# Padding the operand buffers of the matmuls by 32 and 64 bytes in a two-layer hybrid decoder trunk

## The chip, the cores and the metric

The kernel runs on one core of one Trainium2 chip. The metric is device time in microseconds (us) of one execution, from the first to the last instruction, as a median over runs.

## The reference

The reference computes two layers on 512 tokens of width 1,024, all in float32. Layer 0 normalises, projects once, and splits the result between a chunked state space scan (16 heads of 64) and a sliding-window attention (16 query heads, 2 key heads, window 128); both are projected back by one matrix. Layer 1 has a causal convolution module (width 31) in that place. Each layer ends in a gated feed-forward part of width 2,816 with a short convolution between its up-projection and its activation.

```python
def conv_ffn(h, w_up, conv_w, conv_b, w_down):
    u = causal_depthwise_conv(h @ w_up, conv_w, conv_b)
    return (jax.nn.silu(u[..., :D_FF]) * u[..., D_FF:]) @ w_down

for i in range(DEPTH):
    hn = rms_norm(h, mix_norm_w[i])
    if i % 2 == 0:
        proj = hn @ hyb_w_in[j]
        y_a = ssd_mixer(proj[..., :IN_A], ...)
        y_b = swa_sink_attention(proj[..., IN_A:], ...)
        mix = jnp.concatenate([y_a, y_b], axis=-1) @ hyb_w_out[j]
    else:
        mix = conformer_conv_module(hn, ...)
    h = h + mix
    h = h + conv_ffn(rms_norm(h, ffn_norm_w[i]), ffn_w_up[i], ...)
```

## The kernel before

Activations are held transposed: 128 channels on the partitions, 512 tokens along the free dimension, eight such tiles for the width of 1,024. Four phases run in turn, each with a pool of its own for its buffers: mix (layer 0's mixer), ffn0, conf (the convolution module), ffn1. Buffers that all phases use (tags in the set base, L78: wr, wh, wl, xr and some smaller ones) come from a shared pool; sbt (L81) picks the pool and hands out the next buffer of a tag. A tag has a fixed number of buffers of one size, placed one behind the other, and is used in rotation.

Large products keep float32 accuracy with three fast matmuls in place of one. Every operand is split into a rounded high part and the rest: a weight tile of 128 x 1,024 arrives in wr by DMA (wload, L124), ACT writes its high part to wh and DVE the rest to wl (wsplit, L118, three buffers each). Norm.split (L179) does the same for the normalised activations, with 16 buffers xr: high and low of row block 0, then of row block 1, and so on. The feed-forward part writes its gated activations as pairs of g (L782 to L785, 44 buffers). The attention's outputs are pairs of att (L684 to L687, 16 buffers); the state space half's outputs are pairs of xr (L732 to L735).

gemm (L131) runs over the row blocks of one weight tile and issues three matmuls for each:

```python
for i, (xh, xl) in enumerate(ops):
    c = slice(i * P, (i + 1) * P)
    TE.matmul(bank, wh[:, c], xh, start=first and i == 0, stop=False)
    TE.matmul(bank, wh[:, c], xl, start=False, stop=False)
    end = TE.matmul(bank, wl[:, c], xh, start=False, stop=last and i == n - 1)
```

They are lines 136, 137 and 138 of the profile. Each has 128 x 128 weights (the first argument after the bank) and a moving operand of 128 x 512. The up-projections (ffn, L756) use xr and go over 44 weight tiles of eight row blocks per layer; the down-projections use g and have eight output tiles of 22 row blocks per layer. The input projection of the mixer uses xr, its output projection att and then xr. The convolution module uses xr for its first projection and, for its second, dg, pr and g of its own pool (outputs, L1015, and gemm).

The order of work is set by the tile scheduler from the order of the program, with weight loads and splits pulled ahead (L127), except at the start of mix and in conf, where the order is written by hand. DMAs of weights go through SP's queue.

Of the kernel before, what the change touches and what calls it, by code (L numbers as in the profile page):

```python
# [14 lines left out]
P = 128  # L15
# [45 lines left out]
def kernel(ctx: ExitStack, tc: tile.TileContext, x, w_in, w_dt, w_out,  # L61
# [12 lines left out]
    def nm(s):  # L74
        uid[0] += 1
        return f"{s}_{uid[0]}"

    base = {"wr", "wh", "wl", "xr", "nsum", "nsq", "nvar", "nr", "nrb", "cv", "ct", "th"}  # L78
    phase = [sb]

    def sbt(tag, bufs, n=T, dt=F32, shape=None):  # L81
        pool = sb if tag in base else phase[0]
        return pool.tile(shape or [P, n], dt, name=nm(tag), tag=tag, bufs=bufs)

    BANKS = {"mm": 3, "pa": 2, "pb": 2, "pc": 1}
# [20 lines left out]
    def prm(name, i=None, n=1):  # L106
        group, o, w = PARAMS[name]
        t = ptiles[group]
        return t[:, o : o + w] if i is None else t[:, o + i : o + i + n]
# [8 lines left out]
    def wsplit(raw, n):  # L118
        wh, wl = sbt("wh", 3, RING, F32R), sbt("wl", 3, RING, F32R)
        S.copy(wh[:, :n], raw[:, :n])  # L120
        V.tensor_tensor(wl[:, :n], raw[:, :n], f32(wh[:, :n]), op=ALU.subtract)  # L121
        return wh, wl

    def wload(src):  # L124
        n = src.shape[-1]
        raw = sbt("wr", 3, RING)
        with tc.high_priority(offset=AHEAD):  # L127
            nc.sync.dma_start(raw[:, :n], src)
            return wsplit(raw, n)
# [43 lines left out]
    class Norm:  # L173
# [5 lines left out]
        def split(self, k):  # L179
            w = prm(self.wname, k)  # L180
            xh = sbt("xr", 16, T, F32R)
            S.activation(xh, h[k], AF.Copy, scale=w)
            xl = sbt("xr", 16, T, F32R)
            V.scalar_tensor_tensor(xl, h[k], w, f32(xh), op0=ALU.mult, op1=ALU.subtract)
            self.ops[k] = (xh, xl)
# [39 lines left out]
    def mixer(norm, nxt):  # L225
# [81 lines left out]
                V.tensor_copy(dst.rearrange("p j c e -> p c e j"), src.rearrange("p (c e j) -> p c e j", c=NB, e=2))  # L307
            return cs, et, dtj, ddj

        # the first tiles of the projection, fed tile by tile as x arrives  # L310
        first, ws, banks = [], [], {}
        with tc.manual_schedule():
            warm = mk([P, 1], "warm")
# [107 lines left out]
        V.tensor_scalar(nsink, prm("sink"), -1.0, None, op0=ALU.mult)  # L421
        chw = mk([P, 60], "chw")
        V.tensor_scalar(chw, prm("scw", 0, 60), 0.5, None, op0=ALU.mult)
        # convolved channels of the state space heads
        def conv_silu(i, dst):
            v = scaled(proj(), rb)
            t = sbt("ct", 2)
            conv_taps(t, v, None, 0, 4, chw[:, 48 + i : 49 + i], lambda k: chw[:, i * 4 + k : i * 4 + k + 1])
            th = sbt("th", 1)
            S.activation(th, t, AF.Tanh)  # L430
            V.scalar_tensor_tensor(dst, th, 1.0, t, op0=ALU.add, op1=ALU.mult)
# [83 lines left out]
            V.scalar_tensor_tensor(xs[j], xs[j], prm("sd", j), yd, op0=ALU.mult, op1=ALU.add)  # L515
            G.tensor_tensor(xs[j][:, P:], xs[j][:, P:], ec[:, P:], op=ALU.add)

        # keys, values, queries
        kraw = sbt("bc", 4)
        vfm = sbt("bc", 4)  # L520
        qraw = [None] * 8
# [90 lines left out]
            V.tensor_tensor(kla[half], kt[0:64], f32(kha[0:64]), op=ALU.subtract)  # L612
            V.tensor_tensor(klb[half], kt[64:P], f32(khb[64:P]), op=ALU.subtract)

        # attention
        head = {}
        yb = []

# [80 lines left out]
            if i >= LAG:  # L699
                attn_values(*units[i - LAG])  # L700

        # gates
        gs = [sbt("bc", 4) for _ in range(2)]
        for j in range(8):
            v = scaled(proj(), rb)
# [5 lines left out]
            g = j // 4  # L711
# [474 lines left out]
    for i, p in enumerate(phases):  # L1186
        a, b = norms[i], norms[i + 1]
        with tc.tile_pool(name=p, bufs=1) as pool:
            phase[0] = pool
            if p != "mix":  # L1190
                pload(p, pool)
            if p == "mix":
                mixer(a, b)
            elif p == "conf":
                conformer(a, b)
            else:
                l = int(p[-1])
                ffn(a, b, (w_up0, w_up1)[l], (w_dn0, w_dn1)[l], l)
# [105 lines left out]
```

## Time and profile before

| | |
|---|---|
| median of 2 runs | 1336.11 us (1335.57 to 1336.65) |
| profiled execution, its span | 1336.0 us |
| DMA moved | 125.08 MB, mean 94 GB/s |
| mean granted TensorE clock | 0.990 |

The profile gives, for each engine, its busy time, the groups of instructions by source line with their mean duration and the idle time before them, the chain of work that ended last, and a timeline with the start of each instruction. Durations of matmuls overlap, since the next one starts while the present one drains; the distance between two starts is read from the timeline. PE is TensorE's matmul row, PEld its row of weight loads. A tile's name in a row is that of its tag.

### The profile page before, as it was taken

The page shows a single profiled execution, that of the slowest core. Times are in us where ns is not written, and L with a number is a line of the kernel's source. Part 1 is how long each engine was busy: PE and PEld are TensorE (multiplying, and loading weights), DVE is VectorE, ACT ScalarE, POOL GpSimd, SP SyncE. Part 2 cuts the span into 40 slices and gives each one's busy share as a digit, 9 for nine tenths or more (in the row PEclk, how much of TensorE's full clock was granted, in tenths as well). Part 3 has the DMA queues.
Part 4 walks back from the last instruction along what each step waited for, and adds up shares of the span by engine and source line. Part 5 has one row for each costly group of instructions (what it writes and reads, how often), then busy time and mean ns, then how long its engine had stood idle before and what let it go on. Part 6 is the DMA issues. An engine that isn't in the chain of part 4 may idle for free.

```text
span 1336.0 us, 17056 instructions
## 1 busy us (share of the span) xinstructions
PE 1298.3 (97%) x6480; PEld 1040.7 (78%) x6480; DVE 884.8 (66%) x1430; ACT 541.3 (41%) x855; POOL 226.5 (17%) x264
## 2 busy tenths in 40 slices
PE   9999999999999999999999999687999999999998
PEld 7877777778888888888888866556888888888887
DVE  6976759985348777777323368897667777774221
ACT  5465537863234333333222244324633433332120
POOL 0031214540210000000000176672500000000000
PEclk9999999999999999999999999889999999999999
DMA  6212212212333333333233273532232233333331
GB/s 214 96 48 63 64 64 64 64 34 78 95 98 95 95 95 97 99 103 89 87 103 88 87 196 109 133 87 91 79 96 96 95 95 95 96 94 106 104 114 38
DMA packets 41553, 125.08 MB, mean 94 GB/s; under 512 B 4864, under 2 KB 7936, under 8 KB 41472
## 3 DMA queue, kind: packets, MB, share of 16 engines
q1 hardware_dynamic: 40752, 123.46, 30.0%
q8 instruction: 51, 0.84, 0.2%
q10 hardware_dynamic: 720, 0.55, 0.2%
q14 instruction: 30, 0.25, 0.1%
HBM read 119.64 MB, written 4.35 MB: 93 GB/s over the span
## 4 chain that ended last, share of the span: by engine, by line
PE 84%; DVE 9%; POOL 3%; ACT 2%; issue 2%; DMA 1%; POOLq 0%; ACTq 0%; DVEq 0%
PE mm L136 24%; PE mm L137 24%; PE mm L138 24%; DVE g L888 3%; POOL yp L903 1%; PE pb L506 1%; PE pc L681 1%; PE pb L672 1%; DVE wl L851 1%; DVE g L961 1%; PE pa L870 1%; PE pa L137 1%; PE pa L138 1%; PE pa L136 1%; PE pc L513 0%
## 5 line engine op out<-in xcount | busy, mean ns | idle before, releaser
L136 PE MATMUL mm<-xr,wh 128*128 128x512 f32 (+1 forms) x1136 | 442.4, 389 | 0.9 <-ACT wh L847 0.9
L138 PE MATMUL mm<-xr,wl 128*128 128x512 f32 (+1 forms) x1136 | 439.3, 387 | 2.7 <-DVE wl L851 2.7
L137 PE MATMUL mm<-xr,wh 128*128 128x512 f32 (+1 forms) x1136 | 439.4, 387 | 0.0
L120 ACT CAST wh<-wr 128x1024 fp32r<-128x1024 f32 (+1 forms) x178 | 183.6, 1032 | 466.0 <-PE mm L137 422.5
L121 DVE TENSOR_TENSOR wl<-wr,wh 128x1024 fp32r<-128x1024 f32 (+1 forms) x178 | 214.4, 1204 | 163.9 <-ACT wh L120 158.8
L136 PEld LDWEIGHTS mm<-xr,wh 128*128 128x128 f32 x1136 | 214.2, 189 | 47.3 <-issue 4.7
L138 PEld LDWEIGHTS mm<-xr,wl 128*128 128x128 f32 x1136 | 214.1, 189 | 46.3 <-DVE wl L851 2.9
L137 PEld LDWEIGHTS mm<-xr,wh 128*128 128x128 f32 x1136 | 214.3, 189 | 42.1 <-issue 0.6
L137 PE MATMUL mm<-g,wh 128*128 128x512 f32 x368 | 145.0, 394 | 0.0
L222 DVE TENSOR_TENSOR cv<-mm,nrb 128x512 f32<-128x512 f32 x114 | 78.2, 689 | 96.4 <-PE mm L138 91.6
L138 PE MATMUL mm<-g,wl 128*128 128x512 f32 x352 | 138.7, 394 | 0.0
L136 PE MATMUL mm<-g,wh 128*128 128x512 f32 x352 | 138.7, 394 | 0.0
L217 DVE SCALAR_TENSOR_TENSOR ct<-cv,par_ffn,ct 128x510 f32<-128x510 f32 (+1 forms) x176 | 131.0, 747 | 3.5 <-issue 0.4
L194 POOL TENSOR_TENSOR nsum<-nsum,nsq 128x512 f32<-128x512 f32 x21 | 34.0, 1617 | 433.0 <-ACT nsq L193 433.0
L137 PEld LDWEIGHTS mm<-g,wh 128*128 128x128 f32 x368 | 68.8, 187 | 17.0
L136 PEld LDWEIGHTS mm<-g,wh 128*128 128x128 f32 x352 | 65.8, 187 | 16.4
L138 PEld LDWEIGHTS mm<-g,wl 128*128 128x128 f32 x352 | 65.8, 187 | 16.2
L214 ACT ACTIVATE ct<-cv,par_ffn 128x512 f32<-128x512 f32 x88 | 71.4, 813 | 3.2 <-DVE cv L222 3.0
L903 POOL TENSOR_TENSOR yp<-yp,pr 128x512 f32<-128x512 f32 x36 | 59.9, 1664 | 37.4 <-ACT pr L902 35.8
L780 ACT ACTIVATE th<-ct 128x512 f32<-128x512 f32 x44 | 27.8, 632 | 84.5 <-DVE ct L217 84.5
L888 DVE SCALAR_TENSOR_TENSOR g<-u,par_conf,g 128x512 f32<-128x512 f32 x42 | 56.2, 1337 | 1.1
L791 DVE TENSOR_TENSOR h<-h,mm 128x512 f32<-128x512 f32 x16 | 11.0, 688 | 59.1 <-PE mm L138 59.1
(344 smaller groups left out, 1519.4 us busy)
## 6 DMA issues: line engine op xcount, KB each, us to landing
wr<-w_up SPq DMA_DIRECT2D x88, 512.0 KB, 3.5
wr<-w_in SPq DMA_DIRECT2D x29, 512.0 KB, 3.6
wr<-w_dn SPq DMA_DIRECT2D x32, 448.0 KB, 3.3
wr<-pw SPq DMA_DIRECT2D x24, 512.0 KB, 3.6
wr<-w_out SPq DMA_DIRECT2D x16, 512.0 KB, 3.6
wr<-w_dn SPq DMA_DIRECT2D x16, 512.0 KB, 3.5
u<-du SPq DMA_DIRECT2D x24, 262.0 KB, 4.7
u<-du SPq DMA_DIRECT2D x16, 140.0 KB, 2.9
```

Source lines behind the costliest of these rows:

```text
L120: S.copy(wh[:, :n], raw[:, :n])
L121: V.tensor_tensor(wl[:, :n], raw[:, :n], f32(wh[:, :n]), op=ALU.subtract)
L136: TE.matmul(bank, wh[:, c], xh, start=first and i == 0, stop=False)
L137: TE.matmul(bank, wh[:, c], xl, start=False, stop=False)
L138: end = TE.matmul(bank, wl[:, c], xh, start=False, stop=last and i == n - 1)
L194: eng.tensor_tensor(self.sum, self.sum, sq, op=ALU.add)
L214: S.activation(t, v, AF.Identity, bias=bias, scale=w(taps - 1))
L217: V.scalar_tensor_tensor(t[:, s:], v[:, : T - s], w(k), t[:, s:], op0=ALU.mult, op1=ALU.add)
L222: V.tensor_tensor(v, bank, rb, op=ALU.mult)
L780: S.activation(sg, c, AF.Silu)
L888: V.scalar_tensor_tensor(y[j], win(j, k), w(j, k), cvp[j, None] if k == ks[0] else y[j], op0=ALU.mult, op1=ALU.add)
L903: G.tensor_tensor(yp[j], yp[j], pr, op=ALU.add)
```

## The change

sbt adds a few float32 columns to each buffer of five tags, 8 (32 bytes) or 16 (64 bytes), and returns the buffer without them. Buffers of the pool of the convolution module are left as they are; xr, wh and wl come from the shared pool and are padded in every phase. The rest of the diff turns comment lines into empty ones.

```diff
+    STAGGER = {"xr": 8, "g": 8, "att": 8, "wh": 8, "wl": 16}
+
     def sbt(tag, bufs, n=T, dt=F32, shape=None):
         pool = sb if tag in base else phase[0]
+        extra = 0 if pool.name == "conf" else STAGGER.get(tag, 0)
+        if extra and shape is None:
+            return pool.tile([P, n + extra], dt, name=nm(tag), tag=tag, bufs=bufs)[:, :n]
         return pool.tile(shape or [P, n], dt, name=nm(tag), tag=tag, bufs=bufs)
```

## The prediction

> **What bounds the kernel now.** I read the page's busy times, the chain of work that ended last, the groups of instructions by form, and then the timeline for the starts of single matmuls.
>
> ```profile
> PE 1298.3 (97%) x6480; PEld 1040.7 (78%) x6480; DVE 884.8 (66%) x1430; ACT 541.3 (41%) x855; POOL 226.5 (17%) x264
> PE 84%; DVE 9%; POOL 3%; ACT 2%; issue 2%; DMA 1%; POOLq 0%; ACTq 0%; DVEq 0%
> L136 PE MATMUL mm<-xr,wh 128*128 128x512 f32 x1088 | 427.9, 393 | 0.0
> L137 PE MATMUL mm<-g,wh 128*128 128x512 f32 x368 | 145.0, 394 | 0.0
> L137 PE MATMUL mm<-att,wh 128*128 128x512 f32 x48 | 20.2, 422 | 0.0
> L136 PE MATMUL mm<-xr,wh 128*128 128x256 f32 x48 | 14.4, 301 | 0.9 <-ACT wh L847 0.9
> 410.00:610.00 200.00, 200.00 (x884) 165.62 (x883) 156.46 (x205) 78.50 (x93) 0.00 (x0) 1.00 0.32 98
> ```
>
> TensorE is busy 97% of the span and holds 84% of the chain. The last row (busy PE, PEld, DVE, ACT, POOL of 200 us, then the granted clock) shows a stretch of the feed-forward up-projection: TensorE never pauses, DVE is busy 78%. So the time is the number of matmuls times the distance from one start to the next. The 393 ns in the groups is not that distance, because matmuls overlap. The timeline has it:
>
> ```profile
> 499.92 0.39 PE L138 MATMUL mm<-xr,wl 128*128 128x512 f32 x1
> 499.92 0.19 PEld L136 LDWEIGHTS mm<-xr,wh 128*128 128x128 f32 x1
> 500.15 0.39 PE L136 MATMUL mm<-xr,wh 128*128 128x512 f32 x1
> ...
> 501.05 0.39 PE L137 MATMUL mm<-xr,wh 128*128 128x512 f32 x1
> ...
> 689.80 0.39 PE L137 MATMUL mm<-g,wh 128*128 128x512 f32 x1
> ...
> 691.20 0.39 PE L137 MATMUL mm<-g,wh 128*128 128x512 f32 x1
> ...
> 291.00 0.40 PE L138 MATMUL mm<-att,wl 128*128 128x512 f32 x1
> ...
> 296.13 0.39 PE L136 MATMUL mm<-att,wh 128*128 128x512 f32 x1
> ...
> 301.50:306.00 4.50, 4.50 (x12) 3.46 (x11) 4.32 (x12) 2.02 (x4) 0.00 (x0) 0.50 0.17 66
> ...
> 301.32 0.63 PE L138 MATMUL mm<-att,wl 128*128 128x512 f32 x1
> ...
> 306.02 0.63 PE L137 MATMUL mm<-att,wh 128*128 128x512 f32 x1
> ```
>
> Five gaps from 499.92 to 501.05 are 1.13 us, 226 ns at the rows' 10 ns of rounding; the stretch above counts 884 matmuls in 200 us, two of them at its edges, which is 226.7 ns each. Six gaps on g tiles are 1.40 us: 233.3 ns. Twenty-two on att tiles are 5.13 us: 233.2 ns. The shape, the line and the clock (1.00) are the same, so where the operands lie in memory is worth 6.6 ns, 3%. At half the clock (0.50 in the window's row) eleven gaps are 4.70 us, 427.3 ns, and half of that is 213.6 ns: what a matmul would take at full clock with nothing in its way. So 226.7 holds 13 ns of stall and 233.3 holds 20. The weights of the next matmul are read while the present one streams (499.92 beside 499.92).
>
> **Which addresses match.** The compiled program of the kernel before puts xr at byte 47,392 of each partition, wh at 80,160, wl at 92,448, g at 123,360, att at 124,736, and each further buffer 2,048 or 4,096 on. Modulo 256 that is 32, 32, 32, 224 and 64: xr starts where its weights start, g and att do not. The conformer's last products test this with the moving tiles (dg, pr, g, all at 192) left alone and the weights changed:
>
> ```profile
> 947.83 0.39 PE L137 MATMUL mm<-g,u 128*128 128x512 f32 x1
> ...
> 950.55 0.39 PE L137 MATMUL mm<-g,u 128*128 128x512 f32 x1
> ...
> 951.25 0.40 PE L137 MATMUL mm<-g,u 128*128 128x512 f32 x1
> ...
> 956.13 0.40 PE L137 MATMUL mm<-g,u 128*128 128x512 f32 x1
> ...
> 957.05 0.40 PE L138 MATMUL mm<-dg,wl 128*128 128x512 f32 x1
> ...
> 960.57 0.40 PE L138 MATMUL mm<-dg,wl 128*128 128x512 f32 x1
> ...
> 974.42 0.40 PE L137 MATMUL mm<-xr,wh 128*128 128x512 f32 x1
> ...
> 976.51 0.39 PE L137 MATMUL mm<-xr,wh 128*128 128x512 f32 x1
> ...
> 977.87 0.39 PE L137 MATMUL mm<-xr,wh 128*128 128x512 f32 x1
> ```
>
> Weights at 192 too: 12 gaps in 2.72 us, 226.7 ns. Weights at 64: 21 gaps in 4.88 us, 232.4. Weights at 32: 15 gaps in 3.52 us, 234.7. So an equal residue gives 226.7, and the four unequal pairs seen give 232.4 to 234.7, 233.4 in the mean. The last three rows add something: after a break, even the equal pair xr with wh first takes 9 gaps in 2.09 us, 232.2 ns, and only then 6 gaps in 1.36 us, 226.7. The low figure is a rhythm that a row of identical matmuls settles into.
>
> **The change part by part.** No instruction, wait or DMA is added, removed or moved; the slices [:, :n] keep every shape. What moves is where tiles start. (a) xr buffers lie 2,080 bytes apart, so buffer k starts at 32+32k modulo 256; wh (three buffers, b = 0 to 2) at 32+32b, wl at 128+64b. Within one gemm the moving tile now goes +32 (xh to xl), -32 (back), +64 (next row block), so the pair changes at nearly every matmul. For lines 136 and 138 the pair is equal in a quarter of the matmuls at b = 0 and 2 and never at b = 1; for line 137 in a quarter; together about one in five. (b) g, by the same rule, starts at 0+32k in the feed-forward phases, att at 96+32k. (c) Tiles behind wl in the shared pool move on by 800 bytes, 32 modulo 256; the conformer's own u, dg and g keep their distances to one another and shift against wh.
>
> Price of (a), bounds first. Nothing in the trace shows a rotating pair. The best end is the settled 226.7 (no loss), the worst the dearest fixed pair, 234.7. I take 232.2, the row it is nearest to: the pair that has not settled, since a pair that changes each time has no rhythm to settle into. The one equal pair in five is then no relief, for it comes singly. Of the 3,312 matmuls of 512 columns on xr (3 x 1,088, and 48 more in the output projection), 2,112 are the up-projections (88 weight tiles x 24) in unbroken rows at 226.7: 2,112 x 5.5 ns = +11.6 us. The other 1,200 are often broken by small matmuls; nine at 232.2 and fifteen at 226.7 in a tile of 24 would be 228.8 at worst, none broken 226.7; I take 228: 1,200 x 4.2 = +5.0 us. Price of (b): 1,056 matmuls on g (2 x 22 x 24), 233.3 to 232.2, -1.2 us; 192 on att, -0.2 us. The 144 of 256 columns on xr:
>
> ```profile
> 932.28 0.28 PE L1022 MATMUL mm<-pr,wl 128*128 128x256 f32 x1
> 932.39 0.28 PE L1020 MATMUL pc<-pr,xh 128*128 128x256 f32 x1
> ...
> 934.16 0.28 PE L1020 MATMUL mm<-dg,wh 128*128 128x256 f32 x1
> ...
> 935.46 0.28 PE L1022 MATMUL pc<-dg,xl 128*128 128x256 f32 x1
> ```
>
> Eleven gaps in 1.30 us, 118 ns, for a mixed row; against 120 of the equal pair that is -0.3 us. Price of (c): some 50 matmuls of 512 columns and 120 of 256 may change by 7 and 3 ns, 0.7 us either way; nothing taken. DVE, ACT and POOL read and write the same shapes; I cost them at nothing, and should one slow by a few ns, DVE's 22% of idle time in the up-projection row covers it. DMA: the raw tile wr is not padded, so no transfer changes.
>
> Sum: 11.6 + 5.0 - 1.2 - 0.2 - 0.3 = +14.9 us on the profiled execution's span of 1336.0, which agrees with the median of the runs shown, 1336.11. Predicted 1351, +1.1%. What is late next is nothing new: TensorE stays the bound and waits less for others.
>
> [...]
>
> **The rivals.** *No effect*: with the phase averaging out, xr loses what g gains, or the residue acts only in fixed pairs; 1336. Against it stands that xr has three times the matmuls of g and is the one that sits at the low figure. *All settle*: the rotation repeats every four row blocks, so a rhythm could settle for all at 226.7. Then xr keeps its time (the broken 1,200 win 1.3 ns), g wins 6.6 and att 6.5: -1.6 - 7.0 - 1.2 = -9.8 us, 1326. For it: two different absolute residues, 32 and 192, both settled at the same figure. *The stall goes* (faster side): two streams that start apart could miss each other altogether. The shortest gap seen at 256 columns, 932.28 to 932.39, is 0.11 us against 106.8 unstalled (half of 213.6): about 6 ns of stall allowing for the rounding. With 6 on every matmul, 219.6: 2,112 x 7.1 + 1,200 x 8.4 + 1,056 x 13.7 + 192 x 13.6 = 42 us less, and 1 us on the short ones: 1293. It decides for over 2% once the mean gap falls by 5.9 ns over these 4,560. Against it: no pair of 512 columns holds under 226.7. *The dearest pair everywhere* (slower side): 234.7 gives 2,112 x 8.0 + 1,200 x 6.7 + 1,056 x 1.4 + 192 x 1.5 = 26.7 us, 1363; from a mean of 234.7 on it passes 2%. Only one of five rows stands there.
>
> [...]
>
> **How the numbers follow.** Unsettled, 1351: 0.50. No effect, 1336: 0.14. All settle, 1326: 0.14. Stall gone, 1293: 0.16. Dearest pair, 1363 or more: 0.06. Two per cent, about what a measurement of this kernel tells from no change, is 1309 to 1363; so faster 0.16, within 0.78, slower 0.06. The range 1318 to 1362 leaves out the last two cases; the likeliest one's own range is 1341 (half the loss) to 1362.
>
> **What would show it.** In the profile after: the up-projection's gap near 232 and no longer constant from one matmul to the next, the down-projection's (on g) within 1 or 2 ns of 233, instruction counts and every other engine's durations unchanged. The prediction is wrong if the up-projection's gap is at or under 227, or if the g gap falls by more than 5 ns.

## The result and the profile after

The changed kernel takes 1345.33 us (median of 2 runs, 1345.21 to 1345.44) beside 1336.11 before: a ratio of 1.006, with a 95% interval of 1.0041 to 1.0079. That is slower by more than the measurement is uncertain, and inside the 2% that the prediction calls no change. The forecast was 1351, in a range of 1318 to 1362. The profiled execution has a span of 1343.2 us where the one before had 1336.0.

The page of the kernel after has the busy times, the chain by engine, and the groups by form. Every line below the diff stands five lower: 141, 142 and 143 are the three matmuls of gemm.

```profile
PE 1305.5 (97%) x6480; PEld 1038.0 (77%) x6480; DVE 885.5 (66%) x1430; ACT 541.9 (40%) x855; POOL 226.2 (17%) x264
PE 84%; DVE 9%; POOL 3%; ACT 2%; issue 2%; DMA 1%; POOLq 0%; ACTq 0%; DVEq 0%
...
L141 PE MATMUL mm<-xr,wh 128*128 128x512 f32 x1088 | 432.4, 397 | 0.0
...
L142 PE MATMUL mm<-g,wh 128*128 128x512 f32 x368 | 145.1, 394 | 0.0
```

The instruction counts are those of before, the other engines moved by 0.7 us or less, and the chain has the same shares. TensorE's busy time went from 1298.3 to 1305.5, which is the 7.2 us by which the span grew; what it idles is 37.7 us in both (1336.0 - 1298.3, 1343.2 - 1305.5). So TensorE waits no longer than before: the matmuls themselves stand further apart. The mean of a group on xr rose by 4 ns and that of a group on g by none.

The windows of busy time give the distance between starts. In each row the number behind PE's busy time counts the matmuls in the stretch; two at the edges are taken off, as in the prediction, and the result is good to about 0.6 ns. The first row is a stretch of the up-projection of layer 0, the second of the down-projection of layer 1, the third the stretch of the output projection that ran at half clock before. Kernel before, the row that the prediction did not show:

```profile
1210.00:1310.00 100.00, 100.00 (x430) 80.14 (x429) 30.11 (x31) 19.45 (x21) 0.00 (x0) 1.00 0.36 107
```

Kernel after:

```profile
410.00:610.00 200.00, 200.00 (x866) 162.31 (x865) 152.69 (x200) 77.05 (x92) 0.00 (x0) 1.00 0.31 97
1210.00:1310.00 100.00, 100.00 (x433) 80.96 (x432) 33.40 (x38) 21.75 (x23) 0.00 (x0) 1.00 0.36 109
...
301.50:306.00 4.50, 4.50 (x21) 3.68 (x20) 4.50 (x10) 2.49 (x4) 0.00 (x0) 1.00 0.33 110
```

Up-projection: 200 us / 864 = 231.5 ns where it was 226.7. Down-projection: 100 / 431 = 232.0 where 100 / 428 is 233.6 (a mean of 233.3 over all its gaps). The third row has the granted clock at 1.00 where the prediction's had 0.50, and 21 matmuls fit into the 4.5 us where 12 did. Adding up the starts of all matmuls against split weights gives where the 7.2 us came from:

| | before, us | after, us | difference | predicted |
|---|---|---|---|---|
| xr, the 2,112 of the up-projections | 479.5 | 489.2 | +9.7 | +11.6 |
| xr, the other 1,200 | 293.4 | 296.2 | +2.8 | +5.0 |
| g (1,087, with 31 of the convolution module) | 253.6 | 252.1 | -1.5 | -1.2 |
| att, 192 | 49.9 | 47.0 | -2.9 | -0.2 |
| all other matmuls, waits among them | | | -0.9 | -0.3 |

The starts of single matmuls in the trace, matched in order with the addresses of the compiled program, show what the rotation does. These are the last twelve gaps (ns) of three weight tiles of the up-projection, with the residue of wh modulo 256:

```
from 481.9 us, wh at 32:  231 232 230 232 226 229 235 228 229 233 235 233
from 487.5 us, wh at 96:  231 232 234 232 233 230 237 226 231 231 230 230
from 498.6 us, wh at 32:  231 232 230 232 226 229 235 228 229 233 235 233
```

No gap is constant, but the row at 498.6 repeats that at 481.9 gap for gap: the three buffers of wh with 24 matmuls each make one rhythm of 72 matmuls, and its mean is 231.4.

### The profile page after: what moved, and what is told of

It reads as the page before. It is cut to its first block, busy times and chain, and to the rows that moved or that the text cites. A ratio compares the mean times of both kernels' runs of the same rounds, so it can differ in the third digit from the quotient of the medians.

```text
span 1343.2 us, 17056 instructions
## 1 busy us (share of the span) xinstructions
PE 1305.5 (97%) x6480; PEld 1038.0 (77%) x6480; DVE 885.5 (66%) x1430; ACT 541.9 (40%) x855; POOL 226.2 (17%) x264
## 4 chain that ended last, share of the span: by engine, by line
PE 84%; DVE 9%; POOL 3%; ACT 2%; issue 2%; DMA 1%; POOLq 0%; ACTq 0%; DVEq 0%
PE mm L141 24%; PE mm L143 24%; PE mm L142 24%; DVE g L893 2%; POOL yp L908 1%; PE pb L511 1%; PE pc L686 1%; PE pb L677 1%; DVE wl L856 1%; DVE g L966 1%; PE pa L875 1%; PE pa L141 1%; PE pa L143 1%; PE pa L142 1%; PE pc L518 0%
```

## The experiments

Ten kernels were run in three groups, each with the kernel before beside it on the same chip; its medians there were 1336.69 (9 runs), 1338.33 (one run) and 1336.77 us (11 runs). The kernels of sections 2 to 4 ran once each and are read by their gaps, not by their times. "Distance" is the start of the moving operand less the start of the weights that are read under it, modulo 256; these are the weights of the next matmul, as in the prediction's rows at 499.92 us, where the load for L136 starts with the matmul of L138.

### 1. Only the moving operands, only the weights, and everything aligned

The first two do half of the change each. The third pads nothing: an unused tile of 64 bytes ahead of g and one of 224 bytes ahead of att bring both to residue 32, where xr, wh and wl already start.

```diff
# moving operands only
+    STAGGER = {"xr": 8, "g": 8, "att": 8}
# weights only
+    STAGGER = {"wh": 8, "wl": 16}
# everything aligned, as each phase's pool is opened
+            if p != "conf":
+                pool.tile([P, 56 if p == "mix" else 16], F32, name=f"shift_{p}")
```

> Only xr, g and att are padded by 8 columns; wh and wl stay unpadded, all at residue 32 modulo 256. Theory A (the gap depends on the distance, modulo 256 bytes, between the start of the moving operand and the start of the weights read under it, and on whether that distance stays the same long enough to settle): the pair still changes at nearly every matmul, so xr gaps near 231.6 ns as in the changed kernel and g gaps near 232, time 1343 to 1347 us. Rival B (only the step from one moving operand to the next matters): the same, 1345. Rival C (the padding of the weights does the harm): xr back at 226.7, g at 233.3, time 1336.

> Only wh (8 columns) and wl (16 columns) are padded; the moving operands keep one residue each. Theory A: within one weight tile the three pairs repeat, so each tile settles to a pattern of its own; the mean over tiles lies between 229 and 234 ns for xr and for g, time 1340 to 1348 us. Rival B (only the step between moving operands matters): nothing changes, xr 226.7, g 233.3, time 1336. Rival C: as the changed kernel, 1345.

> No buffer is padded; 64 bytes of unused tile ahead of g in the feed-forward phases and 224 ahead of att in the mixer put both at residue 32, where wh and wl are. Theory A: g and att gaps fall from 233.3 to 226.7 ns once settled, 1,056 x 6.6 + 192 x 6.5 = 8.2 us less, time 1327 to 1329 us. Rivals B and C (steps between moving operands, or weights padding): no pad, no step changes, so 1336.

Moving operands only: 1348.97 us (1346.37 to 1349.98), a ratio of 1.0086 (1.007 to 1.0101). Weights only: 1349.35 (1349.1 to 1350.97), 1.0098 (1.0084 to 1.0111). Everything aligned: 1330.77 (1328.56 to 1330.86, 5 runs), 0.9952 (0.9939 to 0.9964): faster than both the kernel before and the changed one. All three medians lie above the times expected of Theory A (1343 to 1347, 1340 to 1348, 1327 to 1329), while their gaps are those it expected. The windows of the three, up-projection and down-projection as above:

```profile
410.00:610.00 200.00, 200.00 (x865) 162.09 (x864) 154.39 (x202) 77.36 (x92) 0.00 (x0) 1.00 0.31 95
```

```profile
410.00:610.00 200.00, 200.00 (x861) 161.30 (x860) 153.44 (x201) 76.28 (x90) 0.00 (x0) 1.00 0.31 95
```

```profile
410.00:610.00 200.00, 200.00 (x884) 165.62 (x883) 156.37 (x204) 77.24 (x92) 0.00 (x0) 1.00 0.32 98
1210.00:1310.00 100.00, 100.00 (x442) 82.78 (x442) 28.40 (x28) 19.60 (x20) 0.00 (x0) 1.00 0.34 104
```

Either half alone brings the whole loss on xr (200 / 863 = 231.7 ns and 200 / 859 = 232.8); the two together cost no more than one. With the moving operands alone the up-projection repeats the same twelve gaps (231, 230, 230, 232, 232, 235, 231, 235, 230, 238, 228, 228), to 1 ns, in nearly every weight tile: a rotating operand settles, into a dearer rhythm (231.7 in the mean). With the weights alone each weight tile has distances of its own, the same for every row block, and 232.3 to 233.2 ns follow. Aligned, g falls to 226.7 by its single starts (the window gives 100 / 440 = 227.3), at 1,056 x 6.6 = 7.0 us the better part of the 9.4 us by which the starts add up to less than before.

### 2. The distance, in steps

If an equal start is what makes 226.7, other fixed distances must give other figures, with nothing rotating. The g tiles get slots of 2,304 bytes (nine times 256) and start inside them at one of three places, by row block, other ones in layer 1.

```diff
+AT = ((32, 40, 8), (16, 48, 20))     # the second kernel: ((17, 18, 28), (14, 12, 36))
...
+            at = AT[l][0 if i < 8 else 1 if i < 15 else 2]
-            gh = sbt("g", 44, T, F32R)
+            gh = sbt("g", 44, T + 64, F32R)[:, at : at + T]
```

gw is cut in the same way.

> g buffers are 2,304 bytes apart and the operand starts at an offset that is the same for all row blocks of one weight tile: distances from the weights of 64, 96 and 224 bytes (modulo 256) for the three weight tiles in layer 0's down-projection and of 0, 128 and 16 in layer 1's. Theory A: the distance 0 settles at 226.7 ns, 128 near 232; 64, 96, 224 and 16 were not seen before and should each settle to a figure of their own between 226 and 236. Rival B: all six at 233.3. Time between 1330 and 1338 us.

> As the scan before, with distances from the weights of 4, 8 and 48 bytes in layer 0's down-projection and of -8, -16 and 80 in layer 1's. Theory A (distance modulo 256): small distances stay near 226.7 ns and the figure climbs with the distance, 48 and 80 between 227 and 234. Theory A2 (A, and the gaps lock to a clock of 6.67 ns that runs on by itself: e4's settled patterns add up to 34, 35, 103 over 3 and 139 over 4 of these): every settled pattern adds up to a multiple of 6.67 ns. Rival (equality of all address bits above the 4 bytes of an element counts): every one of the six at 231 or more.

The timeline of the first, pairs of rows at the two ends of a stretch: distances 64, 96, 224 in layer 0, then 0 and 128 in layer 1.

```profile
687.92 0.39 PE L139 MATMUL mm<-g,wl 128*128 128x512 f32 x1
...
693.19 0.40 PE L138 MATMUL mm<-g,wh 128*128 128x512 f32 x1
...
694.84 0.39 PE L139 MATMUL mm<-g,wl 128*128 128x512 f32 x1
...
697.87 0.39 PE L137 MATMUL mm<-g,wh 128*128 128x512 f32 x1
...
699.72 0.40 PE L139 MATMUL mm<-g,wl 128*128 128x512 f32 x1
...
702.52 0.40 PE L139 MATMUL mm<-g,wl 128*128 128x512 f32 x1
...
1223.79 0.40 PE L139 MATMUL mm<-g,wl 128*128 128x512 f32 x1
...
1226.97 0.39 PE L138 MATMUL mm<-g,wh 128*128 128x512 f32 x1
...
1228.82 0.40 PE L137 MATMUL mm<-g,wh 128*128 128x512 f32 x1
...
1232.09 0.40 PE L139 MATMUL mm<-g,wl 128*128 128x512 f32 x1
```

Distance 64: 23 gaps in 5.27 us, 229.1 ns (the last of them is already at distance 96). Distance 96: 13 in 3.03, 233.1. Distance 224: 12 in 2.80, 233.3. Distance 0: 14 in 3.18, 227.1; by the single starts its first two, 233 and 230, had not settled, and the twelve behind them are 226.7. Distance 128: 14 in 3.27, 233.6. With slots of 2,304 bytes the distance modulo 512 changes by 256 from one g tile to the next, and distance 0 gives 226.7 all the same, while 128 gives 233.6: 256 bytes more made no difference here, 128 more made 6.9 ns. The second kernel, distance 4, then two weight tiles at distance -16:

```profile
690.33 0.40 PE L139 MATMUL mm<-g,wl 128*128 128x512 f32 x1
...
695.30 0.40 PE L139 MATMUL mm<-g,wl 128*128 128x512 f32 x1
...
1231.18 0.39 PE L137 MATMUL mm<-g,wh 128*128 128x512 f32 x1
...
1235.71 0.39 PE L139 MATMUL mm<-g,wl 128*128 128x512 f32 x1
...
1246.62 0.39 PE L138 MATMUL mm<-g,wh 128*128 128x512 f32 x1
...
1251.06 0.39 PE L139 MATMUL mm<-g,wl 128*128 128x512 f32 x1
```

Four bytes off: 21 gaps in 4.97 us, 236.7 ns, the dearest of all, where Theory A expected small distances to stay near 226.7. At -16 one weight tile has 20 gaps in 4.53 us, 226.5, and a later one 19 in 4.44, 233.7. The settled figures, from starts to the nanosecond over each last twelve gaps of a tile:

| distance, bytes | 0 | 4 | 8 | 16 | 48 | 64 | 80 | 96 | 128 | 224 | -16 | -8 |
|---|---|---|---|---|---|---|---|---|---|---|---|---|
| ns | 226.7 | 236.7 | 233.3 | 231.7 | 233.3 | 228.9 | 231.1 | 233.3 | 233.3 | 233.3 | 226.7, 233.3 or 236.7 | 230.0 or 233.3 |

Ten of the twelve distances have one settled figure in all eight output tiles. Two have several: -16 settled at 236.7 in one tile, 226.7 in one and 233.3 in six; -8 at 230.0 in one and 233.3 in seven. So the figure is not a function of the distance alone: the addresses are the same in all eight tiles. What decides between them, no run here shows. Of these twelve, equality is the only distance that caught 226.7 in every tile. The whole runs took 1334.46 and 1338.75 us (one run each), in line with the mean gap over the tiles, 231.4 and 233.4.

### 3. Equal distances with a step between matmuls

The prediction's account needs only equal starts. Here the distance is 0 everywhere in the down-projection, but the low halves (gw, wl) lie further on than the high ones by 32 bytes in layer 0 and 64 in layer 1, so that the pair as a whole steps forward and back. A second kernel does it with 16 and 48 bytes.

```diff
+LOW = (8, 16)                        # the second kernel: (4, 12)
...
+        if tag == "wl":
+            return pool.tile([P, n + 64], dt, name=nm(tag), tag=tag, bufs=bufs)[:, low[0] : low[0] + n]
...
+            gh = sbt("g", 44, T + 64, F32R)[:, 16 : 16 + T]
...
+            gw = sbt("g", 44, T + 64, F32R)[:, 16 + LOW[l] : 16 + LOW[l] + T]
...
+            low[0] = LOW[l]
```

> Every moving operand keeps distance 0 to the weights that are read under it, but the low halves of g and of the weights start 32 bytes (layer 0's down-projection) and 64 bytes (layer 1's) further on than the high halves, so that the moving operand's start steps +32, -32, 0 (+64, -64, 0). Theory A (distance alone): 226.7 ns in both, 1,056 x 6.6 = 7 us less, 1329 to 1331. Rival B (the step from one moving operand to the next counts too): layer 0 at 230 to 233 ns, layer 1 in between or at 226.7.

> As the run with the low halves 32 and 64 bytes on, with 16 bytes in layer 0's and 48 in layer 1's down-projection. Theory A: 226.7 in both. Rival B: both differ from 226.7; by the clock of 6.67 ns the three gaps of a row block add up to a multiple of it, 680, 687 or 693 ns.

The timeline of the first in layer 0, and its window in layer 1:

```profile
689.67 0.40 PE L141 MATMUL mm<-g,wh 128*128 128x512 f32 x1
...
704.77 0.40 PE L140 MATMUL mm<-g,wh 128*128 128x512 f32 x1
```

```profile
1210.00:1310.00 100.00, 100.00 (x435) 81.30 (x434) 29.84 (x31) 19.14 (x20) 0.00 (x0) 1.00 0.36 107
```

65 gaps in 15.10 us are 232.3 ns; the window gives 100 / 433 = 230.9 (231.1 by the single starts). The second kernel has 232.2 and 233.3. No tile settled at 226.7, though every distance is 0. Equal starts are not enough: with these steps from one matmul to the next the gaps were 231.1 to 233.3 ns. (Where every distance is 0, a step is also a distance between the moving operand and its own weights, which were loaded one matmul earlier; the kernels of this section and the next do not tell the two apart.) The runs took 1336.53 and 1335.26 us.

### 4. Moving operand and weights rotate together

The change rotates both by different amounts. Here the high halves of g and the slices of wh go on by 32 bytes together, so that the distance is 0 for two of three matmuls and 32 off for the third; layer 1 does it backwards.

```diff
+STEP = (1, -1)
...
+            part = lambda t, w: t[:, : k * w].rearrange("p (k c) -> p k c", k=k)[:, :, :P]
+            hi = part(wh, P + 8)
...
+            at = (16 + 8 * (i if i < 8 else i - 8 if i < 15 else i - 15)) % 64
+            gh = sbt("g", 44, T + 64, F32R)[:, at : at + T]
```

> Only in the down-projections: the high weights of successive row blocks start 32 bytes further on each time (8 columns of gap in wh), and the high half of g moves with them, so that the operands rotate through all eight multiples of 32 while the pair stays equal under lines 136 and 137 and is 32 bytes apart under 138; layer 1 runs through the row blocks backwards. Theory A (distance alone): two gaps in three at 226.7 and the third between 227 and 233, mean 227 to 229. Rival B (rotation itself does the harm): 231 to 233 as in the changed kernel. The copies of the weights run over blocks of 128 columns with a gap, which may cost ACT and DVE some ns each, hidden.

In layer 0, timeline:

```profile
689.71 0.40 PE L148 MATMUL mm<-g,wh 128*128 128x512 f32 x1
...
704.97 0.40 PE L148 MATMUL mm<-g,wh 128*128 128x512 f32 x1
```

66 gaps in 15.26 us are 231.2 ns; in layer 1 it was 230.8 by the single starts. The run took 1333.62 us. That leaves one form of rotation: a step that is the same from every matmul to the next. The next kernel issues the down-projection in three passes (wh with gh, wh with gw, wl with gh, all row blocks of a weight tile in each) and lays everything out so that both operands go on by 32 bytes each time, back in layer 1.

```diff
+        seq = [(wh[i], ops[i][0]) for i in order] + [(wh[i], ops[i][1]) for i in order] + [(wl[i], ops[i][0]) for i in order]
+        for i, (a, o) in enumerate(seq):
+            TE.matmul(bank, a, o, start=first and i == 0, stop=last and i == len(seq) - 1)
```

> The down-projections are issued in three passes per weight tile (all row blocks of wh with the high halves, then of wh with the low halves, then of wl with the high halves), on weights and buffers laid out so that moving operand and weights start at the same residue in 472 and more of 528 gaps per layer, and both go on by 32 bytes from each matmul to the next in layer 0 and back by 32 bytes in layer 1. Nothing is left out. Theory A (two conditions: equal start residue, and the same residue from one matmul to the next; any step costs): both layers between 230 and 233 ns, like the rotation in step before this (231.1 and 230.8), the span within 1 us of 1333. Rival B (a step that is always the same shifts the beat by a fixed amount, so that one direction waits longer and the other shorter): one layer near 230.0 ns, the other near 223.3, the sum of the two 453; the span near 1332. Rival C (what cost in the rotation before was the return of the pair between the three matmuls of one row block, not the step from block to block): 226.7 in both layers, the span near 1329.

Gaps at distance 0 with an even step were 231.3 ns in the mean forward (488 of them) and 231.2 backward (472). Forward, most of them alternate between two values, one of them short and one long:

```
layer 0: 235 236 230 236 226 236 226 236 226 235 226 236 226 236 225 236
layer 1: 234 228 232 224 233 229 231 233 235 230 231 225 232 230 230 234
```

Each forward pair takes 462 ns, where two gaps of 226.7 would take 453. Theory A stands by the gaps, B and C fall: every step tried from one matmul to the next costs (230.8 to 233.3 ns in this section and the one before), and this one by the same amount in both directions. The order of three passes was not tried without the step. The run took 1332.5 us with a span of 1330.5, under the 1332 to 1334 that A expected; the gaps explain 1,056 x 2.2 = 2.3 us less than before, and the runs of the kernel before beside it had spans of 1333.0 to 1335.9.

### 5. The change without xr, wh and wl

```diff
+    STAGGER = {"g": 8, "att": 8}
```

> The change with only its padding of g and att; xr, wh and wl start where they did before. Theory (the change's whole loss sits in xr with its weights; rotating the moving operand past a fixed weight brings g from 233.3 to what it was with the moving operands alone padded, 231.4): xr gap 227.2, g between 231 and 233, att within 1 of 233; 1,056 x 1.9 = 2.0 us less than before at most, a ratio between 0.998 and 1.000. Rival (the loss of the change comes from padding as such, through the larger pools, spread over all stages): a ratio over 1.002 and xr above 228.

1332.97 us (8 runs, 1331.41 to 1334.53), a ratio of 0.9973 (0.9963 to 0.9984), just under the band that was expected.

```profile
410.00:610.00 200.00, 200.00 (x884) 165.62 (x883) 156.19 (x205) 77.72 (x92) 0.00 (x0) 1.00 0.31 97
1210.00:1310.00 100.00, 100.00 (x434) 81.16 (x433) 27.35 (x27) 19.61 (x20) 0.00 (x0) 1.00 0.35 103
```

The up-projection is back at the count of before, 884. The down-projection is at 100 / 432 = 231.5 ns, and the starts on g add up to 2.1 us less. The loss is that of xr, wh and wl; the larger pools of g and att cost nothing. In the profiled execution att takes 2.7 us less, but nearly all of that goes with the clock: 13 of its gaps over 300 ns lie in a stretch of that of before with the clock at 0.50, 12 of them at 427 ns, and none here. Its gaps under 300 ns fell from 233.7 to 232.5 ns, some 0.2 us over all. Of the gain of 3.8 us in the medians g so explains 2.1 and att some 0.2; the rest stays open. The granted clock of single executions varies between 0.986 and 0.992 in all these kernels.

## Why the prediction was right

*What bounds the kernel.* Right: the whole difference is in the gap between matmul starts, and the idle time of TensorE and the busy time of every other engine stayed.

*The operand addresses set the gap.* Right, and shown by the steps of distance: nothing but 4 bytes of start lie between 226.7 and 236.7 ns. The account given for it, that an equal distance is cheap and an unequal one dear, is half of it. Section 3 has equal distances at 231.1 to 233.3 ns, section 2 an unequal one that caught 226.7 once. In the runs 226.7 came reliably where two things held: equal residues, and no change of residue from one matmul to the next. The kernel before happens to have both on xr.

*"A pair that changes each time has no rhythm to settle into."* This is the step that failed, though the size that it lent was close. That was luck: the 232.2 came from an equal pair that had not settled yet, and nothing in the runs ties that to a rotation. It settles: into twelve gaps with the moving operands alone, into 72 with the change. What was right is that no such rhythm found is as good as 226.7. The mean was 231.4 in the up-projection where 232.2 was taken from an unsettled stretch, so +9.7 us where 11.6 were forecast.

*The 1,200 broken ones on xr.* 2.8 us where 5.0 were taken, though the price of a gap was nearly right: 1,116 of them were under 300 ns before and after, with a mean of 228.2 before (228 was taken) and 232.0 after, and they cost 4.2 us. The other 84, which hold waits and four gaps of 427 ns at the start of the kernel before that were 230 to 238 after, became 1.5 us shorter in total; the prediction had no term for these.

*g.* -1.5 us where -1.2 was forecast, by the same account: a fixed unequal pair replaced by a rotating one. *att.* -2.9 where -0.2 was forecast. Most of it is the stretch from 301.5 us on, with the granted clock at 0.50 before and at 1.00 in this execution; this the prediction had no term for. Its gaps under 300 ns fell from 233.7 to 231.5 ns, some 0.4 us. *Everything else* moved by -0.9.

*The sum.* +7.2 us of span where 14.9 were forecast: 1.9 us too much in the first term, 2.2 in the second, 0.3 in g, 2.7 in att with its clock, 0.6 in the rest. The medians differ by more, 9.2 us: the run that was profiled after took 1345.21 us with a span of 1343.2, 2.0 more, so that a span of 1336.0 before belongs to a run some 2 us over the median of 1336.11. The prediction took the two for the same thing. The mean granted clock was 0.990 in the profiled execution before and 0.992 in the one after; an estimate from these, 0.002 x 1336, puts 2.7 us of difference down to the clock, so the padding costs nearer to the 9.2 us of the medians than to the 7.2.

*The rivals.* No effect (1336) falls with the intervals. All settle at 226.7 (1326) falls for the change. The kernel with everything aligned comes nearer to it: its profiled span is 1326.7, though its median is 5.9 us under that of before and not 9.8. The stall gone (1293) falls: no settled rhythm in any of the kernels is under 226.7. The 213.6 ns that its stall is counted from is an estimate, half of the 427.3 measured at a clock of 0.50; that a matmul with nothing in its way takes as long, no run here shows. The dearest pair everywhere (1363) falls, though a distance of 4 bytes shows a pair dearer than the 234.7 it was priced by.

## What to carry to other kernels

In this kernel TensorE is busy 97% of the span and each matmul reads new weights. Where the operands of successive matmuls started at the same residue modulo 256, moving tiles and weights alike, the gap was 226.7 ns; an unused tile at the start of three pools was enough to bring g there, and worth 0.5% (1330.77 beside 1336.69 us). In a kernel like it this layout is the one to try first; here it was measured at 128 x 128 weights with 512 columns alone. Rotating the starts gave means of 230.8 to 232.8 ns in every form tried, dearer than that and within the 228.9 to 236.7 of the unequal fixed distances that settled at one figure. Where a layout in use already has the equal case, as xr had here, padding for the sake of rotation takes it away: 226.7 became 231.4. Read the loss from the distance between starts, not from the mean duration of the groups: on g that mean stayed at 394 ns while the gap fell from 233.3 to 231.9.

## What was not expected of the hardware

The settled rhythms add up to whole numbers of 6.667 ns: 226.67 is 34 of them, 233.33 is 35, three gaps of distance 64 (686.7) are 103, four of distance 16 (926.7) are 139, two of distance 4 (473.3) are 71, three of distance 80 (693.3) are 104, and the 72 of the change (16,660) are 2,499. In the kernel before, 3,797 starts stand in rows of five gaps of 226 to 227 or of 233 to 234 ns. Taken modulo 6.667 ns, 3,787 of them lie within 0.6 ns of the mean of their 100 us, and that mean drifts by some 2 ns over the whole 1.3 ms. Theory A2 expected such sums; the clock that it puts behind them, and why a step of the address shifts the starts, no run here shows. At a granted clock of 0.50 the gap is 426.7 ns by the single starts, twelve of them from 301.3 us on in the kernel before (the prediction's 427.3 has the rounding of the rows); half of that is 213.3. How much of a stall is left in it, no run here shows.
